# A sample's value products in one piece, or in four pieces spread over four units of the attention loop

## The chip, the cores and the metric

The kernel runs on one core of a Trainium2 chip. The metric is the device time of one execution, in microseconds (us). A core has a matrix engine (TensorE, PE in the profile, with its weight loads listed apart as PEld), three engines for elementwise work (VectorE or DVE, ScalarE or ACT, GpSimd or POOL), a queue engine (SyncE or SP), and 16 DMA engines. Each engine runs its own instructions strictly in order; between engines they wait on semaphores. TensorE writes only to PSUM, an accumulator memory of 8 banks of 2 KB per partition, which DVE and ACT read. SBUF is the working memory.

## The reference

One layer of a streaming encoder, run for a prompt of 2048 frames and for 8 samples of 16 new frames each. Attention has 8 heads of 64 channels. A prompt frame sees its own chunk of 64 frames and the 8 chunks before; a sample's frame sees 256 cached keys and the 16 new ones. What matters here, cut to its core:

```python
s = jnp.einsum("bqhd,bkhd->bhqk", qc, kc) * scale + bias
p = jax.nn.softmax(jnp.where(valid, s, NEG_INF), axis=-1)
att = jnp.einsum("bhqk,bkhd->bqhd", p, vc)          # the value products
...
y = jnp.concatenate([att, c], axis=-1) @ w_out      # c: the convolution branch
x = x + rmsnorm(y, g_mix_post)
```

Cross-attention into 256 memory tokens and a gated feed-forward layer follow, for both groups. The outputs are the new frames and the updated caches.

## The kernel before

The program goes through memory keys and values, the input projection with the convolution, attention, the output projection with cross-attention, and the feed-forward layer. The change is in attention (about 645 to 945 us).

The prompt is cut into 16 tiles of 128 frames. The loop of `attention` goes over 128 units, one for each head (8) and tile (16), and at unit i it issues, in this order:

- `scores` of unit i (L847): products of the tile's queries with up to five key blocks, in four matmuls, into one of two "s" places in PSUM. DVE adds the bias and finds the maximum (`softmax_band`, L761), ACT takes the exponential (L763). The first tiles of a head have fewer blocks: 128 columns for tile 0, 256 for tile 1 and so on, 640 from tile 4.
- `transp` of unit i - 4 (L864): the probabilities of that unit are transposed on TensorE, in groups of up to four blocks, each group into one of three "t" slots in PSUM (one bank each). ACT copies the group to its high part (L865), DVE subtracts to get the low part (L866); then the slot is free.
- `values` of unit i - 6, every fourth unit (L877): the value products of four tiles, 16 matmuls of 128 to 512 columns, into the single "o" place, emptied by ACT (L881) and DVE (L883).
- at some units, one step of `sample`: the attention of one of the 8 samples over all heads, written as a generator whose pieces end at each `yield`.

A sample's steps are: load cached keys, cached values and new values from SP (L768, L770, L772); transpose the keys in two steps (L780, copied by ACT at L781); POOL copies the new keys behind them (L783); scores (L794, eight heads at once in 128 rows) with softmax and a normalisation on POOL (L798); transposes of the probabilities (L803); and the value products (L812, L813). The value products go over four pairs of heads: for each pair there are two blocks of cached values and one of new values, and the moving operand, the probabilities of the pair, is only 32 columns wide. In the profile each pair takes four matmul instructions of L812 and two of L813, so a sample has 24. All four pairs share one "o" tile, which two copies on DVE empty (L815, L816) into `attS`.

A sample belongs to a head: sample h starts its steps at tile 0 of head h, and a step is taken at every second unit (2, 4, ... 14), for the last head at every unit from its sixth tile on (`SLAST`). The value products come at unit 14, in the last head at tile 9.

The order on each engine is not just the order of the code. A planner goes through the instructions when the program is built, in simulated time: on each engine the earliest instruction in the code whose inputs and places are ready goes first, so a step of a sample can be hoisted ahead of its unit or slip behind it. The order so found is then fixed. `issue_after` adds an order edge: instructions of the block come behind a named one on the same engine.

The output projection (`mixout`) begins with the sample tile, which needs `attS` complete: its high and low parts are made by `prep` (L1003, L1004) and multiplied at L289. Only then come the 16 prompt tiles. The weights of the output projection are loaded during the last head into places that attention gives up, among them a buffer of cached keys and one of cached values.

Of the kernel before, what the change touches and what calls it, by code (L numbers as in the profile page):

```python
# [8 lines left out]
F32 = mybir.dt.float32  # L9
# [8 lines left out]
P = 128  # L18
D = 1024
KC = D // P  # L20
NPT = 16
S_TILE = 16
H = 8
DH = 64
# [5 lines left out]
DEC_B = 8  # L30
DEC_S = 16
# [5 lines left out]
WEIGH = (122, 124)  # L37
FROM = 2
F2 = 2
SLAST = NPT * (H - 1) + 4  # L40
MID = 4
TR0 = [12, 8]
MM = [12, 14, 4, 6]
# [93 lines left out]
class Build:  # L137
# [605 lines left out]
    def attention(self):  # L743
        nc, A = self.nc, self.A
# [13 lines left out]
        def softmax_band(ps, w, bias, sm):  # L758
            z = self.t(pool, [P, W5], F32, "z", 6)
            nmx = self.t(pool, [P, 1], F32, "nmx", 12)  # L760
            nc.vector.tensor_tensor_reduce(out=z[:, :w], in0=ps, in1=bias, scale=-1.0, scalar=3e38,  # L761
                                           op0=ALU.add, op1=ALU.min, accum_out=nmx[:, :])
            nc.scalar.activation(z[:, :w], z[:, :w], AF.Exp, bias=nmx[:, :], scale=-1.0, accum_out=sm)  # L763
            return z

        def sample(s):
            kc = self.t(pool, [P, 2, 512], F32, "kc", 2)
            nc.sync.dma_start(kc[:, :, :], A["cache_att_k"][s].rearrange("(b p) d -> p b d", p=P))  # L768
            vc = self.t(pool, [P, 2, 512], F32, "vc", 2)
            nc.sync.dma_start(vc[:, :, :], A["cache_att_v"][s].rearrange("(b p) d -> p b d", p=P))  # L770
            vn = self.t(pool, [DEC_S, 512], F32, "vn", 2)
            nc.sync.dma_start(vn[:, :], self.vsamp[s * DEC_S:(s + 1) * DEC_S, :])  # L772
            yield
            kt = self.t(pool, [P, 4, PAST + DEC_S], F32, "kt", 1)
            for c2 in range(0, 4, 2):
                pt = self.t(ps_t, [P, 2, 2, P], F32, "t")
                for c in range(2):
                    for b in range(2):
                        cc = slice((c2 + c) * P, (c2 + c + 1) * P)
                        nc.tensor.transpose(pt[:, c, b, :], kc[:, b, cc], self.ident[:, :])  # L780
                nc.scalar.copy(kt[:, c2:c2 + 2, :PAST].rearrange("p c (b k) -> p c b k", k=P), pt[:, :, :, :])  # L781
                yield
            nc.gpsimd.tensor_copy(kt[:, :, PAST:], self.ksamp[:, :, s * DEC_S:(s + 1) * DEC_S])  # L783
            yield
            qb = qbds[s % 2]
            for o in range(2):
                rr = slice(o * DH, (o + 1) * DH)
                nc.vector.tensor_copy(qb[rr, :, o * DEC_S:(o + 1) * DEC_S],
                                      self.qsamp[rr, :, s * DEC_S:(s + 1) * DEC_S])
            qb = qb[:, :, :].rearrange("p c x -> p (c x)")  # L790
            n = PAST + DEC_S
            ps = self.t(ps_s, [P, 2, 512], F32, "s")[:, 0, :n]
            for c in range(4):
                nc.tensor.matmul(ps, qb[:, c * P:(c + 1) * P], kt[:, c, :], start=c == 0, stop=c == 3)  # L794
            sm = self.t(pool, [P, 1], F32, "sm", 2)
            z = softmax_band(ps, n, bs[:, :], sm[:, :])
            nc.vector.reciprocal(sm[:, :], sm[:, :])
            nc.gpsimd.tensor_scalar(z[:, :n], z[:, :n], sm[:, :], None, ALU.mult)  # L798
            yield
            pt = self.t(ps_t, [P, 3, P], F32, "t")  # L800
            for b in range(3):
                w = P if b < 2 else DEC_S
                nc.tensor.transpose(pt[:w, b, :], z[:, b * P:b * P + w], self.ident[:, :])  # L803
            pp = self.t(pool, [P, 3, P], F32, "pp", 1)
            nc.scalar.copy(pp[:, :2, :], pt[:, :2, :])
            nc.scalar.copy(pp[:DEC_S, 2, :], pt[:DEC_S, 2, :])
            yield
            po = self.t(ps_o, [P, 4, 32], F32, "o")
            for c in range(4):
                cc, hc = slice(c * P, (c + 1) * P), slice(c * 32, (c + 1) * 32)  # L810
                for b in range(2):
                    nc.tensor.matmul(po[:, c, :], vc[:, b, cc], pp[:, b, hc], start=b == 0, stop=False)  # L812
                nc.tensor.matmul(po[:, c, :], vn[:, cc], pp[:DEC_S, 2, hc], start=False, stop=True)  # L813
            ss = slice(s * DEC_S, (s + 1) * DEC_S)
            nc.vector.tensor_copy(self.attS[:DH, :, ss], po[:DH, :, :DEC_S])  # L815
            nc.vector.tensor_copy(self.attS[DH:, :, ss], po[DH:, :, DEC_S:])  # L816

        def load_head(h):

            jj, odd = h // 2, h % 2  # L820
            rr = slice(odd * DH, (odd + 1) * DH)
            q2 = self.t(pool, row, F32R, f"q2{odd}", 1)
            k2 = self.t(pool, row, F32R, f"k2{odd}", 1)
            kl = self.t(pool, row, F32R, f"kl{odd}", 1)
            v2 = self.t(pool, [P, NPT, P], F32R, f"v2{odd}", 1)
            nc.gpsimd.dma_start(q2[:, :], self.qs[jj][rr, :, :].rearrange("d c n -> (d c) n"))
            for c, dst in ((0, k2), (1, kl)):
                nc.gpsimd.dma_start(dst[:, :], self.ks[jj][c, rr, :].unsqueeze(1).to_broadcast([DH, 2, NPT * P]))
            nc.gpsimd.dma_start(v2[:, :, :], self.vs[h // 4][:, h % 4, :, :])
            bt = self.t(pool, [P, W5], F32, "bt", 2)  # L830
            nc.sync.dma_start(bt[:, :], toep[h][:, :])
            nc.gpsimd.memset(bt[:DH, W5 - DH:], NEG)
            nc.gpsimd.memset(bt[DH:, :DH], NEG)
            return q2, k2, kl, v2, bt
# [15 lines left out]
        def transp(zs, t, quad):  # L850
            if t % 4 == 0:
                quad = [self.t(pool, [P, 20, P], F32R, f"p{c}{t // 4 % 2}") for c in "hl"]
            ph, pl = quad
            if t < 4:
                chunks = [(5 * t + 4 - t, 5 * t + 5)]
            else:
                x = t % 4
                chunks = [(4 * x, 4 * x + 4)] + ([(16, 20)] if x == 3 else [])
            for a, b in chunks:
                pt = self.t(ps_t, [P, 4, P], F32, "t")  # L860
                for x in range(a, b):
                    u = t - t % 4 + x // 5
                    k = x % 5 - max(0, 4 - u)
                    nc.tensor.transpose(pt[:, x - a, :], zs[u][:, k * P:(k + 1) * P], self.ident[:, :])  # L864
                nc.scalar.copy(ph[:, a:b, :], pt[:, :b - a, :])  # L865
                nc.vector.tensor_tensor(pl[:, a:b, :], pt[:, :b - a, :], ph[:, a:b, :].bitcast(F32), ALU.subtract)  # L866
            return quad
# [24 lines left out]
        for _ in range(2):  # L892
            qb = self.t(pool, [P, 4, P + 2 * DEC_S], F32, "qbd")
            nc.gpsimd.memset(qb[:, :, :], 0.0)
            qbds.append(qb)
        fill = iter(())
        self.wo_load = self.out_weights()
        zq, quads = {}, {}
        n = len(units)
# [2 lines left out]
        for i in range(n + LV + 1):  # L902
            if i < n:
                h, t = units[i]
                if t == 0:
                    fill = sample(h)
                if t == 6 and h + 1 < H:
                    heads[h + 1] = load_head(h + 1)
                zq[h, t] = scores(heads[h], t, self.sums[:, t, h:h + 1])
            u = i - LT  # L910
            if 0 <= u < n:
                h, t = units[u]
                quads[u // 4] = transp({x: zq.get((h, x)) for x in range(t - t % 4, t + 1)}, t, quads.get(u // 4))
            u = i - LV
            if 0 <= u < n and u % 4 == 3:
                h, t = units[u]
                values(h, heads[h], t - 3, quads.pop(u // 4))
            if i % NPT and (i % 2 == 0 or i > SLAST):
                next(fill, None)
            if i == n - NPT:  # L920
                self.selectors()
            if i in WEIGH:
                for _ in self.weigh(WEIGH.index(i), ps_t, "t"):
                    pass
            if i in (n - 13, n - 11, n - 9, n - 7):
                next(self.wo_load)
# [771 lines left out]
```

## Time and profile before

| | before |
|---|---|
| median of 3 runs | 3012.31 us (3011.44 to 3014.95) |
| the profiled execution, its own time | 3017.42 us |
| its span, first to last instruction | 3015.6 us |
| TensorE busy | 2946.0 us (98%) |
| weight loads busy | 2712.9 us (90%) |
| DVE / ACT / POOL busy | 71% / 45% / 47% |
| mean granted TensorE clock | 0.989 |
| matmuls at L812 / L813 / L864 | 128 / 64 / 560 |

The profile is of one execution. A busy TensorE in it is not TensorE at its peak, since matmuls are pipelined and their ends are modelled; two things tell more: the share of the weight loads, and the granted clock, which falls to one half in some stretches. A row of a group names the line, the engine, the operation, what it writes and reads with their shapes, the count after an x, the busy time with the mean length of one in ns, and the engine's idle time just before them with what ended it. A row of waits names who waited for whom, the sum in us, how often, and the longest. A row in order of time has the start, the length, and the instructions merged in it.

### The profile page before, as it was taken

What the parts mean: (1) busy time and instruction counts of PE and PEld (TensorE: products, weight loads), DVE (VectorE), ACT (ScalarE), POOL (GpSimd) and SP (SyncE); (2) the same over time, 40 slices, a digit from 0 to 9 for tenths busy, and PEclk for the clock granted to TensorE, in tenths of its full rate; (3) what the DMA queues carried; (4) which work ended last, traced back from release to release, by engine and by line L of the source; (5) the groups of instructions that cost most, each with busy time, mean ns of one, the idle gap of its engine ahead of it and who ended that gap; (6) DMA issues with size and microseconds to landing.
All of it is one profiled execution on the core that took longest, in us unless ns stands there. A gap on an engine that the chain in (4) does not pass through costs nothing.

```text
span 3015.6 us, 46098 instructions
## 1 busy us (share of the span) xinstructions
PE 2946.0 (98%) x16924; PEld 2712.9 (90%) x16924; DVE 2137.0 (71%) x3086; ACT 1358.3 (45%) x2729; POOL 1418.9 (47%) x1338
## 2 busy tenths in 40 slices
PE   7999999979999999999999999999999999999998
PEld 7999999969998888788878999999999999888887
DVE  6697795857786466535357887888788999655566
ACT  4535365657785345323334333433334444433433
POOL 1267496721113234226356655555555775524413
PEclk9999999989899999999999999999999999999999
DMA  8635353644534556324246433444434445756674
GB/s 295 246 112 179 96 165 110 202 167 172 181 135 153 175 190 216 128 68 147 74 166 210 138 128 132 166 166 153 154 125 160 144 139 187 260 187 207 220 230 149
DMA packets 197695, 500.10 MB, mean 166 GB/s; under 512 B 19349, under 2 KB 84765, under 8 KB 188627
## 3 DMA queue, kind: packets, MB, share of 16 engines
q1 hardware_dynamic: 182539, 427.53, 42.9%
q0 software_dynamic: 14928, 69.61, 6.2%
q8 instruction: 133, 2.18, 0.3%
q14 instruction: 95, 0.78, 0.1%
HBM read 365.97 MB, written 141.81 MB: 168 GB/s over the span
## 4 chain that ended last, share of the span: by engine, by line
PE 38%; DMA 4%; DVE 3%; issue 3%; POOL 3%; ACT 0%; SPq 0%; DVEq 0%; POOLq 0%; ACTq 0%
PE psb L283 12%; PE psb L282 12%; PE psb L281 12%; DMA sbf<-in_w_down_dram 2%; POOL sbf L1538 1%; PE psb L289 1%; DMA sbf<-x 1%; PE psb L1393 1%; DVE sbr L1416 0%; DMA sbf<-in_w_gate_dram 0%; DVE sbr L1608 0%; POOL sbf L338 0%; DMA hn<-sbf 0%; DVE sbr L1542 0%; DVE flexb L1478 0%
## 5 line engine op out<-in xcount | busy, mean ns | idle before, releaser
L281 PE MATMUL psb<-sbr 128*128 128x384 f32 (+3 forms) x2808 | 942.6, 337 | 4.1 <-DVE flexb L426 1.4
L282 PE MATMUL psb<-sbr 128*128 128x384 f32 (+3 forms) x2356 | 806.2, 342 | 3.4 <-DVE sbr L318 3.3
L283 PE MATMUL psb<-sbr 128*128 128x512 f32 (+3 forms) x1848 | 632.8, 344 | 3.7 <-DVE sbr L1608 3.6
L281 PEld LDWEIGHTS psb<-sbr 128*128 128x128 f32 x2808 | 530.9, 189 | 33.9 <-DVE flexb L426 2.1
L283 PE MATMUL psb<-sbr,sbx 128*128 128x384 f32 (+2 forms) x1484 | 477.2, 322 | 0.0
L282 PEld LDWEIGHTS psb<-sbr 128*128 128x128 f32 x2356 | 445.5, 189 | 30.6 <-DVE sbr L318 3.6
L283 PEld LDWEIGHTS psb<-sbr 128*128 128x128 f32 x1848 | 348.0, 189 | 33.2 <-DVE sbr L1608 6.3
L289 PE MATMUL psb<-sbr 128*128 128x512 f32 x1200 | 295.3, 394 | 2.7 <-POOL sbr L1251 1.4
L1416 DVE TENSOR_TENSOR sbr<-sbf,sbr 128x512 fp32r<-128x512 f32 x258 | 262.5, 1020 | 38.6 <-ACT sbr L1415 37.7
L1415 ACT CAST sbr<-sbf 128x512 fp32r<-128x512 f32 x258 | 159.3, 620 | 278.7 <-PE psb L282 228.8
L283 PEld LDWEIGHTS psb<-sbr,sbx 128*128 128x128 f32 x1484 | 281.2, 190 | 0.1
L523 DVE SCALAR_TENSOR_TENSOR psb<-sbf,psb 128x768 f32<-128x768 f32 (+1 forms) x290 | 264.3, 911 | 6.2
L289 PEld LDWEIGHTS psb<-sbr 128*128 128x128 f32 x1200 | 222.2, 189 | 48.5 <-POOL sbr L1251 1.8
L1608 DVE TENSOR_TENSOR sbr<-sbf,sbr 128x384 fp32r<-128x384 f32 (+2 forms) x242 | 166.4, 711 | 93.6 <-ACT sbr L1607 92.4
L276 POOL TENSOR_TENSOR sbx<-sbf,sbr 128x1024 fp32r<-128x1024 f32 x62 | 158.7, 2563 | 79.9 <-ACT sbr L275 76.4
L1607 ACT CAST sbr<-sbf 128x384 fp32r<-128x384 f32 (+2 forms) x242 | 112.4, 483 | 171.6 <-PE psb L282 149.4
L1538 POOL TENSOR_TENSOR sbf<-sbf 128x512 f32<-128x512 f32 x77 | 107.0, 1392 | 165.5 <-DMA sbf<-in_w_down_dram 163.6
L533 POOL TENSOR_TENSOR flexb<-flexb,flexb 128x128 f32<-128x128 f32 (+1 forms) x180 | 169.4, 942 | 23.1 <-ACT flexb L532 12.3
L281 PE MATMUL psb<-sbr,sbx 128*128 128x384 f32 (+1 forms) x524 | 170.6, 327 | 1.5 <-ACT sbx L1415 0.8
L1415 ACT CAST sbx<-sbf 128x512 fp32r<-128x512 f32 x153 | 94.7, 620 | 162.2 <-PE psb L282 147.4
L1416 DVE TENSOR_TENSOR sbx<-sbf,sbx 128x512 fp32r<-128x512 f32 x153 | 155.3, 1016 | 16.3 <-ACT sbx L1415 16.0
L1410 POOL TENSOR_TENSOR sbf<-sbf 128x512 f32<-128x512 f32 x66 | 96.9, 1468 | 107.3 <-DVE sbr L1416 50.5
(339 smaller groups left out, 6269.2 us busy)
## 6 DMA issues: line engine op xcount, KB each, us to landing
af<-flexb SPq DMA_DIRECT2D x33, 1344.0 KB, 5.7
sbf<-in_w_down_dram SPq DMA_DIRECT2D x154, 256.0 KB, 3.8
sbf<-in_w_gate_dram SPq DMA_DIRECT2D x66, 512.0 KB, 3.5
sbf<-in_w_up_dram SPq DMA_DIRECT2D x66, 512.0 KB, 3.9
sbf<-af SPq DMA_DIRECT2D x85, 384.0 KB, 4.1
sbf<-x SPq DMA_DIRECT2D x49, 512.0 KB, 4.0
sbf<-in_w_in_dram SPq DMA_DIRECT2D x48, 512.0 KB, 4.1
sbr<-ks POOLq DMA_DIRECT2D x16, 1024.0 KB, 8.5
```

The costliest lines, as they stand in the source:

```text
L276: self.lo_engine.tensor_tensor(lo[:, :], wf[:, :], hi[:, :].bitcast(F32), ALU.subtract)
L281: nc.tensor.matmul(ps, lh, rh, start=start, stop=False, **kw)
L282: nc.tensor.matmul(ps, lh, rl, start=False, stop=False, **kw)
L283: nc.tensor.matmul(ps, ll, rh, start=False, stop=stop, **kw)
L289: nc.tensor.matmul(y[o], l, r[:, o * 512:(o + 1) * 512], start=start and x == 0, stop=stop and x == 2)
L523: nc.vector.scalar_tensor_tensor(acc if w < CW - 1 else o, src(w), cwt[:, j, w:w + 1], acc, ALU.mult, ALU.add)
L533: nc.gpsimd.tensor_tensor(o, o, v, ALU.add)
L1415: nc.scalar.copy(hs[j][:, :], src[j])
L1416: nc.vector.tensor_tensor(ls[j][:, :], src[j], hs[j][:, :].bitcast(F32), ALU.subtract)
L1538: nc.gpsimd.tensor_tensor(acc[:, :], acc[:, :], q[:, :], ALU.add if s > 0 else ALU.subtract)
L1607: nc.scalar.copy(ch[:, m], a[:, x, m])
L1608: nc.vector.tensor_tensor(cl[:, m], a[:, x, m], ch[:, m].bitcast(F32), ALU.subtract)
```

## The change

The value products of a sample are cut into four parts, one per pair of heads, and each part is a step of its own. A part has its own accumulator of 32 columns, and it is no longer in the "o" place but takes the next of the three "t" slots, which it shares with the transposes. It is put behind the last transposes that were issued so far (`last_turn`), and two copies on DVE, a quarter as wide as before, empty it.

The steps of sample s are now taken at fixed units counted from the first unit of its head: 1, 7, 8, 9, 11, 13, 14, 15 and 16, the same for every head. The four parts come at 13, 14, 15 and 16; the last one is in the first unit of the next head, and for the last sample it is in the first pass of the loop after all scores. The load of the cached values moves from the first step to the end of the second transposes, and POOL's copy of the new keys joins that step, since one `yield` is gone.

```diff
-SLAST = NPT * (H - 1) + 4
+SAMPLE_AT = (1, 7, 8, 9, 11, 13, 14, 15, 16)
...
-            vc = self.t(pool, [P, 2, 512], F32, "vc", 2)
-            nc.sync.dma_start(vc[:, :, :], A["cache_att_v"][s].rearrange("(b p) d -> p b d", p=P))
             vn = self.t(pool, [DEC_S, 512], F32, "vn", 2)
...
-                yield
+                if c2 == 0:
+                    yield
             nc.gpsimd.tensor_copy(kt[:, :, PAST:], self.ksamp[:, :, s * DEC_S:(s + 1) * DEC_S])
+            vc = self.t(pool, [P, 2, 512], F32, "vc", 2)
+            nc.sync.dma_start(vc[:, :, :], A["cache_att_v"][s].rearrange("(b p) d -> p b d", p=P))
             yield
...
-            po = self.t(ps_o, [P, 4, 32], F32, "o")
+            ss = slice(s * DEC_S, (s + 1) * DEC_S)
             for c in range(4):
                 cc, hc = slice(c * P, (c + 1) * P), slice(c * 32, (c + 1) * 32)
-                for b in range(2):
-                    nc.tensor.matmul(po[:, c, :], vc[:, b, cc], pp[:, b, hc], start=b == 0, stop=False)
-                nc.tensor.matmul(po[:, c, :], vn[:, cc], pp[:DEC_S, 2, hc], start=False, stop=True)
-            ss = slice(s * DEC_S, (s + 1) * DEC_S)
-            nc.vector.tensor_copy(self.attS[:DH, :, ss], po[:DH, :, :DEC_S])
-            nc.vector.tensor_copy(self.attS[DH:, :, ss], po[DH:, :, DEC_S:])
+                po = self.t(ps_t, [P, 32], F32, "t")
+                with self.tc.issue_after(self.last_turn.ins):
+                    for b in range(2):
+                        nc.tensor.matmul(po[:, :], vc[:, b, cc], pp[:, b, hc], start=b == 0, stop=False)
+                    nc.tensor.matmul(po[:, :], vn[:, cc], pp[:DEC_S, 2, hc], start=False, stop=True)
+                nc.vector.tensor_copy(self.attS[:DH, c, ss], po[:DH, :DEC_S])
+                nc.vector.tensor_copy(self.attS[DH:, c, ss], po[DH:, DEC_S:])
+                if c < 3:
+                    yield
...
-                    nc.tensor.transpose(pt[:, x - a, :], zs[u][:, k * P:(k + 1) * P], self.ident[:, :])
+                    self.last_turn = nc.tensor.transpose(pt[:, x - a, :], zs[u][:, k * P:(k + 1) * P],
+                                                         self.ident[:, :])
...
-                if t == 0:
-                    fill = sample(h)
...
-            if i % NPT and (i % 2 == 0 or i > SLAST):
-                next(fill, None)
+            for s in range(DEC_B):
+                if i - NPT * s in SAMPLE_AT:
+                    next(samples.setdefault(s, sample(s)), None)
```

More of the change, by code (lines that the diff above doesn't have):

```diff
@@ L895, in attention @@
             qbds.append(qb)
-        fill = iter(())
+        samples = {}
         self.wo_load = self.out_weights()
```

## The prediction

> **What bounds the kernel now.** I read the page's slices first, because they place the edited stage; this row is the clock that TensorE was granted, in tenths of full speed, over 40 equal slices.
>
> ```profile
> PEclk9999999989899999999999999999999999999999
> ```
>
> The ninth and the eleventh slice (603 to 679 and 754 to 829 us) are the only ones under nine tenths, and they lie at the start of the attention loop and in it. Next, the sums over the steady part of that loop (columns: length, then PE, weight loads, DVE, ACT and POOL busy with their counts, granted clock, DMA share, GB/s) and what PE waited for in it.
>
> ```profile
> 676.00:945.00 269.00, 267.13 (x1750) 248.31 (x1751) 205.15 (x481) 205.88 (x469) 41.18 (x58) 0.94 0.43 155
> PE psb L877 <- DVE sbf L883: 1.4, 1, 1.4
> ```
>
> PE is busy 267 of 269 us and its longest wait is 1.4 us, while DVE and ACT are each free for about 64 us. So PE sets the pace here, and anything that makes PE slower costs time directly. The clock of 0.94 says what does: six stretches at half clock. They stand first below, with two full-clock stretches for comparison.
>
> ```profile
> 685.32:692.15 6.83, 6.83 (x27) 6.17 (x28) 2.00 (x6) 2.07 (x6) 0.29 (x2) 0.50 1.05 406
> 722.87:726.28 3.41, 3.41 (x14) 3.02 (x15) 1.77 (x6) 1.24 (x3) 0.29 (x2) 0.50 0.72 252
> 757.00:760.41 3.41, 3.41 (x17) 3.31 (x16) 2.34 (x6) 1.92 (x5) 0.29 (x2) 0.50 0.90 330
> 787.72:794.54 6.82, 6.82 (x28) 6.30 (x29) 2.68 (x8) 2.38 (x6) 0.29 (x2) 0.50 0.74 279
> 821.85:828.68 6.83, 6.83 (x29) 6.34 (x29) 2.96 (x8) 3.06 (x7) 0.29 (x2) 0.50 0.89 339
> 917.42:920.84 3.42, 3.42 (x16) 3.34 (x16) 2.88 (x12) 2.72 (x7) 0.00 (x0) 0.50 0.48 153
> 692.15:717.00 24.85, 24.85 (x174) 23.40 (x174) 21.51 (x50) 21.57 (x49) 3.50 (x6) 1.00 0.34 113
> 828.68:852.00 23.32, 23.32 (x162) 22.06 (x162) 19.39 (x49) 19.06 (x45) 3.50 (x6) 1.00 0.24 80
> ```
>
> All lengths are 3.41 us or twice that, so the clock is decided in windows of 3.41 us: nine windows, 30.72 us in all. To see what decides, I compared the forms of the matmuls in two windows. After the first (681.91 to 685.32, sample 0) the clock was halved; after the second (855.98 to 859.39, sample 5) it was not.
>
> ```profile
> L812 PE MATMUL psb<-sbf,flexb 128*128 128x32 f32 x9 | 1.5, 278 | 0.0
> L847 PE MATMUL psb<-sbr 128*128 128x256 f32 x6 | 1.2, 302 | 0.0
> L813 PE MATMUL psb<-sbf 16*128 16x32 f32 x4 | 0.8, 282 | 0.0
> L864 PE MATMUL psb<-ident,flexb 128*128 128x128 f32 x4 | 0.7, 286 | 0.0
> L847 PE MATMUL psb<-sbr 128*128 128x128 f32 x2 | 0.4, 302 | 0.2 <-DVE flexb L761 0.2
> ```
>
> ```profile
> L812 PE MATMUL psb<-sbf,flexb 128*128 128x32 f32 x9 | 1.5, 281 | 0.0
> L813 PE MATMUL psb<-sbf 16*128 16x32 f32 x6 | 1.2, 282 | 0.0
> L847 PE MATMUL psb<-sbr 128*128 128x512 f32 x2 | 0.7, 447 | 0.0
> L864 PE MATMUL psb<-ident,flexb 128*128 128x128 f32 x4 | 0.6, 272 | 0.0
> L847 PE MATMUL psb<-sbr 128*128 128x384 f32 x2 | 0.6, 379 | 0.0
> ```
>
> Count by width: 9x32 + 6x256 + 4x32 + 4x128 + 2x128 = 2720 columns in the window that was followed by half clock, and 9x32 + 6x32 + 2x512 + 4x128 + 2x384 = 2784 in the one that was not. My reading is that a window with too few streamed columns halves the next one, with the border near 2750. The sample's value products (L812 and L813) are 24 matmuls of only 32 columns, and they run in one burst. The rows of PE in order around the burst of sample 6:
>
> ```profile
> 885.73 0.63 PE L864 MATMUL psb<-ident,flexb 128*128 128x128 f32 x4
> 886.11 0.59 PE L847 MATMUL psb<-sbr 128*128 128x128 f32 x3
> 886.54 0.60 PE L864 MATMUL psb<-ident,flexb 128*128 128x128 f32 x4
> 886.89 0.71 PE L847 MATMUL psb<-sbr 128*128 128x256 f32 x4
> 887.45 0.60 PE L864 MATMUL psb<-ident,flexb 128*128 128x128 f32 x4
> 887.80 0.60 PE L847 MATMUL psb<-sbr 128*128 128x384 f32 x2
> 888.23 0.53 PE L812 MATMUL psb<-sbf,flexb 128*128 128x32 f32 x4
> ...
> 891.71 0.66 PE L864 MATMUL psb<-ident,flexb 128*128 128x128 f32 x4
> ```
>
> The burst lasts 891.71 - 888.23 = 3.48 us, as long as a window, for 24x32 = 768 columns. Where it fills a window, the clock falls.
>
> **The change part by part.** *Splitting the products.* PE's work stays: 24 matmuls per sample, now four parts of six, each 3.48 / 4 = 0.87 us, each held behind the transposes of its own unit. From 885.73 to 888.23 PE streams 512+384+512+1024+512+768 = 3712 columns in 2.50 us, 1485 per us, and this is a lean place, with the short scores of the next head. A window with one part has 3.41 - 0.87 = 2.54 us left for this and holds 2.54 x 1485 + 192 = 3964; one with two parts has 1.67 us left and holds 1.67 x 1485 + 384 = 2864. Both lie above 2784, the second by little, so I expect most drops to go and a few to stay.
>
> What the drops cost: the six stretches held 27+14+17+28+29+16 = 131 matmuls. At full clock 174+162 = 336 took 48.17 us, 6.98 per us, so 131 would take 18.8 us. Loss now: 30.72 - 18.8 = 12.0 us, or 1.33 us per window. Gain if all go: -12.0. I leave two windows, one in the first head, where PE is also held by other work, and one in the last, where no further head fills the units: +2.7. Bounds: none left, 0, and all nine left, +12.0.
>
> [...]
>
> *Accumulators in the three "t" slots instead of "o".* The parts now rotate with the transposes, whose slots are released by ACT's copy and DVE's subtraction. Rows for what a slot wait costs now, for the copies that empty an accumulator, and for the time to land of a cache load:
>
> ```profile
>   DVE sbr L866: 0.3, 1
> DVE sbf L815 <- PE psb L813: 12.8, 7, 3.7
> L815 DVE COPY sbf<-psb x8: 206/216/218, 688.4 to 917.4; 64x64 f32<-64x64 f32 x8
> DMA to landing us min/median/max: 3.5/4.5/5.8
> ```
>
> The transposes waited 0.3 us in one case for a slot. Four more users per sample bring a slot back a place earlier, but the part itself adds 0.87 us to the turn. I take +0.6 us, twice the 0.3, being nearest that row. Bounds: 0, since the shared "o" slot is given up in return and may repay it, and 32 parts at about 0.25 us, the length of one copy, +8.
>
> *Copies out.* 64 instead of 16, a quarter as wide; no row shows 16 columns, so each lies between 0 and 0.22 us. The 48 added ones cost at most 48 x 0.22 = 10.6 us of DVE, hidden by DVE's 64 free us; without that cover, +10.6. DVE waits for each part with the next scores' reduction (L761) queued behind, and ACT's exponential behind that; it now waits 12.8 us for seven bursts and would wait for shorter pieces. Taken at 0.
>
> *Loads and moved steps.* The key and new-value loads go a unit earlier. The value load goes behind the transposes and POOL's key copy; on SP it is held by its buffer until the sample two before has finished its last part, so it still lands (4.5 us) most of a head before use, and the next head's bias table behind it on SP has as long. For samples 0 and 1 the buffer is free early. POOL's copy is in one step with the second transposes; POOL is busy 41 of 269 us. Score and softmax move one unit earlier with two units still between them and the probabilities' transposes. All 0; if a first value load were late, at most its 5.8 us.
>
> *The last sample.* Its products finished with tile 9 of the last head; now the last part follows the transposes of tile 12. The output projection begins with the sample tile and needs them. Rows of the tail:
>
> ```profile
> 921.74 1.17 PE L289 MATMUL psb<-sbr 128*128 128x512 f32 x4
> ...
> 925.81 4.82 PE L289 MATMUL psb<-sbr 128*128 128x512 f32 x20
> ...
> 932.11 0.60 PE L864 MATMUL psb<-ident,flexb 128*128 128x128 f32 x4
> ```
>
> These 24 projection matmuls, 1.17 + 4.82 = 6.0 us, run before the transposes of tile 12 (932.11) and fill PE while the head drains. They will have to come after. The four parts, 3.48 us, move into the place: 6.0 - 3.5 = +2.5 us of hole. Bounds: 0, if tile 12 simply comes earlier, and +6.0.
>
> *Sum.* -12.0 + 2.7 + 0.6 + 0 + 2.5 = -6.2 us. The profiled execution took 3017.4 us, 5.1 above the median of 3012.3, with drops whose places depend on where the windows fall; I apply the difference to the median: 3006.1, and say 3006.
>
> **The rivals.** *The waits eat it (about the same).* The slots cost the +8: -12.0 + 2.7 + 8 + 2.5 = +1.2, 3013.5. For it: a slot is released only when DVE is through, and DVE is busy 205 of 269 us. Against: the 0.3 us above.
>
> *The parts bunch (no effect).* If the order of issue lets parts pile up behind a late transpose, windows still fill and the drops stay: +0.6 + 2.5 = +3.1, 3015.4. Against: each part is held behind a different unit.
>
> *The clock falls more often (slower).* The four parts spread over some 7 us with transposes and short scores between. If such windows fall under the border, two per sample follow at half clock: 8 x 6.83 = 54.6 us, a loss of 54.6 x 12.0 / 30.72 = 21.3 instead of 12.0, so +9.3 + 0.6 + 2.5 = +12.4, 3024.7. It decides once a two-part window streams under 2750 columns; 2864 is near. It would be certain if transposes did not count: of the 3712 columns 1536 are theirs, leaving 870 per us, 1.67 x 870 + 384 = 1840 in a two-part window against 2720 - 512 = 2208 in the one that halved. [...]
>
> *Everything goes and the tail closes.* -12.0, 3000.
>
> **How the numbers follow.** 0.2%, 6 us, is about what a measurement can tell from no change. Forecast, with 3002 to 3006 most likely of it and the clean gain to 3000: 0.53. Waits eat it, or the forecast lands short of 6 us: 0.27. Parts bunch: 0.08. Slower: 0.12. So faster 0.53, same 0.35, slower 0.12. The range runs from 2999 (the clean gain, 1 us spare) to 3015 (bunched): about 0.12 lies above, 0.06 below.
>
> **What would show it.** Right: no stretch of 0.50 between 692 and 900 us or at most two, windows with at most 12 narrow matmuls, PE near 100% busy, the loop about 10 us shorter. Waits of L864 or the parts on DVE's copies would show the first rival; stretches of 0.50 over 40 us in sum, the slower one; a gap on PE of over 3 us after the last transposes, a worse tail. A reordered loop with PE idle in it, which I cannot see from here, would make the whole sum wrong.

## The result, and the profile after

The changed kernel took 3021.04 us (median of seven runs, 3019.56 to 3025.03), the kernel before, in turns with it on the same chip, 3012.09 us (seven runs, 3010.07 to 3018.95). The ratio is 1.0027 (1.0015 to 1.004): slower by 9 us, outside the predicted range and of the other sign.

The first row of the page to compare is the granted clock in 40 slices, for the changed kernel:

```profile
PEclk9999999989998999999999999999999999999999
```

The slice from 754 to 829 us is repaired, and there is a new low one, the thirteenth (907 to 982 us). To see this in numbers I cut both traces at the same matmuls, counted from the start: number 4200 lies in the first head, number 5700 near the start of the last, number 6050 in the output projection. Sums over the two stretches, of before and then of after (columns as in the prediction):

```profile
666.33:894.48 228.15, 225.63 (x1501) 210.86 (x1501) 175.39 (x421) 175.97 (x410) 29.34 (x53) 0.94 0.45 161
894.48:954.77 60.29, 60.03 (x352) 52.10 (x351) 47.18 (x87) 42.45 (x85) 16.61 (x11) 0.97 0.41 140
```

```profile
666.31:885.91 219.60, 216.90 (x1502) 198.74 (x1501) 179.52 (x462) 175.53 (x409) 26.94 (x52) 1.00 0.46 164
885.91:957.12 71.21, 67.31 (x351) 57.49 (x351) 48.31 (x96) 43.32 (x89) 19.29 (x13) 0.88 0.38 130
...
913.25:916.67 3.42, 2.08 (x15) 1.66 (x13) 3.29 (x3) 1.68 (x4) 2.35 (x1) 1.00 0.00 0
916.67:933.74 17.07, 16.73 (x63) 14.75 (x64) 10.26 (x20) 8.27 (x13) 2.37 (x1) 0.50 0.57 199
```

The loop is 8.6 us shorter, without any half clock; the last head and the start of the output projection are 10.9 us longer, with one stretch of half clock of 17.07 us, five windows, begun by a window in which PE was busy for only 2.08 of 3.42 us. The rows of PE there, in order:

```profile
913.27 0.61 PE L868 MATMUL psb<-ident,flexb 128*128 128x128 f32 x4
913.72 0.53 PE L815 MATMUL psb<-sbf,flexb 128*128 128x32 f32 x4
914.17 0.40 PE L816 MATMUL psb<-sbf 16*128 16x32 f32 x2
914.51 0.86 PE L882 MATMUL psb<-sbr 128*128 128x128 f32 x3
917.01 1.11 PE L868 MATMUL psb<-ident,flexb 128*128 128x128 f32 x4 [1.64 <-DVE sbr L871]
...
920.07 0.90 PE L815 MATMUL psb<-sbf,flexb 128*128 128x32 f32 x4
...
923.75 0.90 PE L815 MATMUL psb<-sbf,flexb 128*128 128x32 f32 x4
...
927.45 0.90 PE L815 MATMUL psb<-sbf,flexb 128*128 128x32 f32 x4
...
931.97 2.23 PE L289 MATMUL psb<-sbr 128*128 128x512 f32 x5
```

In the order of the program's text the transposes are now L868, the parts L815 and L816, the prompt's value products L882. The eighth sample's four parts lie between 913.72 and 929 us, and not one matmul of the output projection (L289) comes before 931.97. In the kernel before (a second trace of it, introduced below) the same place reads:

```profile
913.52 1.18 PE L289 MATMUL psb<-sbr 128*128 128x512 f32 x4
...
917.61 4.79 PE L289 MATMUL psb<-sbr 128*128 128x512 f32 x20
...
923.33 0.70 PE L289 MATMUL psb<-sbr 128*128 128x512 f32 x2
...
926.00 2.45 PE L289 MATMUL psb<-sbr 128*128 128x512 f32 x10
```

These 36 stood in the drain of the last head. All belong to the sample tile, which takes 48 of them (six for each of eight pieces of the weights). They are 512 columns wide; what is left in their place are transposes of 128, parts of 32 and the prompt's value products of 128 to 512.

The wait of 1.64 us in the low window can be followed to its cause. DVE's subtraction (L1008, one of `prep`, for the convolution half of the sample tile) ran beside a subtraction of POOL (L276), and DVE's release of a "t" slot (L871) stood behind it; the last row groups 17 such L1008:

```profile
913.47 2.89 DVE L1008 TENSOR_TENSOR sbr<-flexb,sbr 128x512 fp32r<-128x512 f32 x1
916.28 0.68 DVE L871 TENSOR_TENSOR sbr<-psb,sbr 128x512 fp32r<-128x512 f32 x1
```

```profile
913.45 2.35 POOL L276 TENSOR_TENSOR sbr<-sbf,sbr 128x1024 fp32r<-128x1024 f32 x1 [3.85 <-PE psb L851]
```

```profile
L1008 DVE TENSOR_TENSOR sbr<-flexb,sbr x17: 673/693/2886, 913.5 to 1179.4; 128x512 fp32r<-128x512 f32 x17
```

Its median is 693 ns; 2886 is POOL's 2.35 us and then one of its own length, less 0.15. POOL's was first by 0.02 us. In the first traces of the two kernels this subtraction occurs 68 times (L1004, L1008). The eight that took over 2 us (2.44 to 2.89) all began while POOL was in an instruction of 1024 columns (L276; L1047 before, L1051 after), and ended 0.55 us after it; the three that began 0.09 to 0.22 us ahead of such a one took 0.68 to 0.69 us. This long subtraction is not new. In the second trace of the kernel before it is L1004:

```profile
916.37 2.89 DVE L1004 TENSOR_TENSOR sbr<-flexb,sbr 128x512 fp32r<-128x512 f32 x1
```

There PE had matmuls of L289 to run meanwhile and lost at most 0.3 us in the whole tail. In the run without the dependency, below, its like takes 2.87 us too, and L289 runs beside it. What is new in the changed kernel is that PE has nothing else to do meanwhile.

### The profile page after: what moved, and what is told of

Read it like the earlier page. It is cut to its first block, busy times and chain, and to the rows that moved or that the text cites. A ratio compares the mean times of both kernels' runs of the same rounds, so it can differ in the third digit from the quotient of the medians.

```text
span 3023.2 us, 46142 instructions
## 1 busy us (share of the span) xinstructions
PE 2945.7 (97%) x16924; PEld 2706.7 (90%) x16924; DVE 2144.3 (71%) x3134; ACT 1359.4 (45%) x2729; POOL 1420.8 (47%) x1338
## 4 chain that ended last, share of the span: by engine, by line
PE 38%; DMA 4%; DVE 3%; issue 3%; POOL 2%; ACT 0%; SPq 0%; POOLq 0%; DVEq 0%; ACTq 0%
PE psb L283 12%; PE psb L282 12%; PE psb L281 12%; DMA sbf<-in_w_down_dram 2%; PE psb L289 2%; POOL sbf L1542 1%; DMA sbf<-x 1%; PE psb L1397 1%; DMA sbf<-hn 0%; DMA sbf<-in_w_gate_dram 0%; DVE sbr L1612 0%; DVE sbr L1420 0%; POOL sbf L338 0%; DVE sbr L1546 0%; DVE sbx L1420 0%
## 5 line engine op out<-in xcount | busy, mean ns | idle before, releaser
L289 PE MATMUL psb<-sbr 128*128 128x512 f32 x1200 | 296.3, 395 | 1.9 <-ACT sbr L1290 1.1
L289 PEld LDWEIGHTS psb<-sbr 128*128 128x128 f32 x1200 | 223.0, 189 | 48.1 <-ACT sbr L1290 1.3
L276 POOL TENSOR_TENSOR sbx<-sbf,sbr 128x1024 fp32r<-128x1024 f32 x62 | 158.8, 2564 | 78.5 <-ACT sbr L275 74.7
```

The source lines that it names most:

```text
L276: self.lo_engine.tensor_tensor(lo[:, :], wf[:, :], hi[:, :].bitcast(F32), ALU.subtract)
L289: nc.tensor.matmul(y[o], l, r[:, o * 512:(o + 1) * 512], start=start and x == 0, stop=stop and x == 2)
```

## The experiments

Each was run in turns with the kernel before, which had medians of 3012.37, 3012.77 and 3013.59 us in the three sets of runs; ratios are against the one beside it.

**The last sample, added alone.** The kernel before, with the eighth sample alone as in the changed kernel (units 1, 7, 8, 9, 11, 13 to 16, four parts; `sample_split` is the changed kernel's `sample`):

```diff
-                    fill = sample(h)
+                    fill = sample(h) if h < H - 1 else iter(())
...
+            if i == NPT * (H - 1):
+                late = sample_split(H - 1)
+            if i - NPT * (H - 1) in SAMPLE_AT:
+                next(late, None)
```

> The kernel before with only the last sample as in the changed one: samples 0 to 6 keep their bursts, sample 7 is in four parts at units 13 to 16 of the last head. Theory A: the loss alone, 3019 to 3025 us, with several windows at half clock after 910 us and the drops of samples 0 to 4 still there. Rival B: within 3 us of before, 3009 to 3015 us.

3018.88 us, ratio 1.0022 (1.001 to 1.0033). The last head and tail, and the half clock in it:

```profile
887.04:955.48 68.44, 65.00 (x352) 56.39 (x352) 46.55 (x93) 41.96 (x86) 18.94 (x12) 0.90 0.34 118
917.35:931.00 13.65, 13.65 (x55) 12.47 (x55) 7.29 (x16) 6.98 (x10) 1.54 (x1) 0.50 0.52 195
```

The last sample alone costs 6.5 us of the 9, in the place expected.

**The last sample, taken out of the change.** The reverse: the changed kernel with the eighth sample as before (`sample_burst` is the `sample` of the kernel before, `LAST_AT` its units 2, 4, 5, 6, 7, 8 and 9).

```diff
+                last = s == DEC_B - 1
-                if i - NPT * s in SAMPLE_AT:
-                    next(samples.setdefault(s, sample(s)), None)
+                if i - NPT * s in (LAST_AT if last else SAMPLE_AT):
+                    next(samples.setdefault(s, sample_burst(s) if last else sample(s)), None)
```

> The changed kernel, with the eighth sample alone as it was before: its value products in one burst in the "o" place at tile 9 of the last head, its steps at units 2, 4, 5, 6, 7, 8 and 9 of that head. Theory A (the split repairs the loop, and the last sample gives it all back in the tail): the part from the last head's scores to the output projection takes 59 to 62 us with at most 4 us of half clock, as before; the loop ahead of it stays at about 220 us without half clock; the time is 3006 to 3010 us, below the kernel before. Rival B (what is lost is not the last sample's, but the new order of the loop or its load of the value cache shifts all that follows): 3017 us or more.

3015.62 us, ratio 1.001 (1.0 to 1.002). The time lies between the two theories. Its loop, and its last head and tail:

```profile
666.90:885.88 218.98, 216.61 (x1501) 198.79 (x1501) 179.71 (x462) 175.67 (x409) 26.94 (x52) 1.00 0.46 165
885.88:949.85 63.97, 62.16 (x352) 53.69 (x352) 47.46 (x90) 43.17 (x87) 19.91 (x13) 0.95 0.39 141
```

So 5.4 us of the 9 come back (3021.04 - 3015.62), but it stays 2.9 above the kernel beside it. The run above gives 6.5 for the same step, so some two thirds of the loss are the last sample's. The loop is as short as in the changed kernel; the tail is still some 3.7 longer than before (63.97 against 60.29), and the projection then waits, in one case 1.9 us, for DVE to empty an accumulator:

```profile
PE psb L290 <- DVE flexb L1104: 2.1, 2, 1.9
PE psb L935 <- ACT sbr L923: 1.0, 1, 1.0
```

Why the planner's order comes out worse there, with the last sample as before, is open.

**Is it the dependency?** The sample tile of the projection no longer reads the samples' attention:

```diff
-                att = self.attS[:, :, :]
+                att = ct[:, :, :]
```

> The changed kernel, but the sample tile of the output projection reads the convolution half in the place of the attention half, so the samples' attention is still computed in full and not used: nothing of the output projection waits for the last part any more. Theory A2 (the loss is that the sample tile has to wait for the last part, and its 24 matmuls are missing where the last head drains): the sample tile starts near 912 to 922 us, the tail takes 59 to 62 us with at most 4 us of half clock, and the time is 3006 to 3011. Rival A1 (the narrow parts alone starve the windows): the half clock in the tail stays at 10 us or more, and the time at 3016 or more.

3014.31 us, ratio 1.0005 (0.9995 to 1.0014), and no half clock left from the loop to the tail:

```profile
665.41:884.60 219.19, 216.63 (x1501) 198.72 (x1501) 179.48 (x462) 175.65 (x409) 26.95 (x52) 1.00 0.45 165
884.60:948.51 63.91, 59.89 (x351) 50.61 (x351) 45.89 (x96) 42.60 (x87) 20.31 (x13) 1.00 0.40 141
...
L289 PE MATMUL psb<-sbr x48: 387/392/497, 909.0 to 934.8; 128*128 128x512 f32 x48
```

The parts are as narrow and as late as in the changed kernel, but L289 starts at 909 us and runs among them. So the half clock in the tail comes from the projection's matmuls being held back by the dependency. The tail still has 4.0 us without a matmul (63.91 - 59.89) where before had 0.3, so it is 63.9 and not the 59 to 62 expected, and the time was 3 us above the window expected.

**The last sample's steps earlier.** The changed kernel, its eighth sample moved forward, four parts at units 9 to 12:

```diff
+LAST_AT = (2, 4, 5, 6, 8, 9, 10, 11, 12)
...
-                if i - NPT * s in SAMPLE_AT:
+                if i - NPT * s in (SAMPLE_AT if s < DEC_B - 1 else LAST_AT):
```

> The changed kernel with only the last sample's steps earlier: loads at unit 2 of the last head, keys at 4 and 5, scores at 6, probabilities at 8, the four parts at 9, 10, 11 and 12 (as changed: 13 to 16). Theory A, the last sample: the change gains about 8 us in the loop and loses about 11 us after the last scores, because the parts and the sample tile of the output projection come too late there; with the parts early the 17 us at half clock around 917 to 934 us are gone or down to one window, the projection's first matmul comes by 924 us, and the time is 3003 to 3010 us. Rival B, the split itself (slots shared with the transposes, 48 more copies, a reordered loop) is what costs: the time stays at 3017 us or more.

3020.15 us, ratio 1.0028 (1.0018 to 1.0038): a miss. The sample tile starts at 921.9 us and the half clock shrinks to one window in each of two stretches, but waits take its place. Last head and tail, and the stretch after it, which took 32.7 us in the changed kernel:

```profile
884.49:950.98 66.49, 61.49 (x351) 52.26 (x351) 47.02 (x95) 43.43 (x88) 17.89 (x12) 0.97 0.39 135
950.98:988.41 37.43, 34.70 (x151) 27.98 (x150) 14.70 (x24) 11.50 (x24) 12.40 (x17) 0.95 0.44 145
```

PE has 5.0 and 2.7 us without a matmul in them. What the tail loses is not the clock alone.

**The slots.** The changed kernel, its parts in the "o" place:

```diff
-                po = self.t(ps_t, [P, 32], F32, "t")
+                po = self.t(ps_o, [P, 32], F32, "o")
```

> The changed kernel with the four parts' accumulators in the single o place again, in place of the three t slots. If the shared slots cost anything (bound in the prediction: 8 us), this is faster than the changed kernel by that, 3013 to 3019 us. By theory A the slots cost next to nothing and the last sample is as late as before: 3019 to 3024 us; slower than the changed kernel where a part has to wait for the place that the four tiles' value products hold.

3021.83 us, ratio 1.003 (1.0019 to 1.0041): no gain. The loop took 217.0 us (219.6 with the "t" slots), the tail 70.2 against 71.2, but matmul 4200 came 2.9 us later (669.19 against 666.31), ahead of any part (the first is matmul 4299). So the loop is some 2 us shorter without the shared slots, and the whole time is not: by the medians the slots don't decide.

**Wider parts.** The changed kernel, each part streaming all 128 probabilities, of which the copies take what counts:

```diff
-                        nc.tensor.matmul(po[:, :], vc[:, b, cc], pp[:, b, hc], start=b == 0, stop=False)
+                        nc.tensor.matmul(po[:, :], vc[:, b, cc], pp[:, b, :], start=b == 0, stop=False)
```

> The changed kernel, with each part's matmuls streaming all 128 probabilities instead of 32; the copies take the two 16 columns that count, nothing else differs. Theory A1 (the tail's half clock comes from windows with few streamed columns): the 17 us of half clock in the tail shrink to 7 or less and the time falls to 3011 to 3016 us. Rival A2 (the tail loses time because the sample tile of the output projection comes late, whatever is streamed): half clock and time as in the changed kernel, 3019 to 3023.

3026.87 us, ratio 1.0044 (1.0031 to 1.0057). Both theories missed: slower than the changed kernel.

```profile
668.39:890.61 222.22, 219.81 (x1501) 198.81 (x1500) 179.85 (x462) 175.98 (x410) 27.30 (x53) 1.00 0.45 162
890.61:962.08 71.47, 65.14 (x352) 54.82 (x351) 48.77 (x96) 42.74 (x88) 20.67 (x13) 0.93 0.37 127
923.05:933.29 10.24, 10.24 (x37) 8.84 (x37) 3.81 (x9) 3.90 (x5) 0.00 (x0) 0.50 0.50 198
```

The half clock is shorter, 10.24 us in place of 17.07, as the columns say, but the tail is not: 6.3 us are without a matmul. In the loop, which had no half clock to lose, the wider parts cost 2.6 us.

**Columns, with the burst left whole.** The same widening in the kernel before, to 128 and to 64:

```diff
-            po = self.t(ps_o, [P, 4, 32], F32, "o")
+            po = self.t(ps_o, [P, 4, P], F32, "o")
...
-                    nc.tensor.matmul(po[:, c, :], vc[:, b, cc], pp[:, b, hc], start=b == 0, stop=False)
+                    nc.tensor.matmul(po[:, c, :], vc[:, b, cc], pp[:, b, :], start=b == 0, stop=False)
```

> The kernel before, bursts and all, but each value matmul of a sample streams all 128 columns of the probabilities in place of the 32 of its pair of heads; the accumulator has 4 times the columns, and the same two copies pick out those that are wanted. The burst streams 3072 columns in place of 768 and should take the same 3.5 us, since each matmul takes 0.145 us now and its weight load, not its 32 columns, sets that. Theory C, streamed columns decide the clock, border near 2750 in a window: no drop at any sample, 12 us less, 2999 to 3004 us. Rival D, something else in the burst decides (narrow matmuls as such, transposes, waits): the drops stay, 3010 to 3015 us, or more if wide matmuls take longer.

> The kernel before with the sample's value products streaming 64 probabilities instead of 32 or 128; the burst then holds 1536 columns. At 128 columns the loop had 3.4 us of half clock and the time was 0.9989 of before; the products took 172 ns each there against 145. If the border lies well above 1536 plus what fits beside it, half clock stays in the loop, 10 us or more, and the time is that of before, 3011 to 3014; if 64 columns are enough, the half clock goes and the products cost less than at 128: 3006 to 3009.

At 128 columns 3010.03 us, ratio 0.9989 (0.998 to 0.9997), faster than the kernel before; at 64, 3015.40, ratio 1.0011 (1.0001 to 1.0021). The loops of the two traces, 128 and then 64:

```profile
664.24:885.65 221.41, 218.85 (x1501) 200.77 (x1501) 175.59 (x423) 175.89 (x411) 29.39 (x53) 0.99 0.46 166
```

```profile
662.95:883.21 220.26, 217.66 (x1501) 202.47 (x1501) 174.38 (x421) 175.79 (x410) 29.43 (x53) 0.98 0.46 166
```

TensorE's matmuls come in the same order in these traces as in those of the kernel before; the burst left whole loses its half clock when more columns pass, so it was the columns. The one halved window left at 128 columns follows a wait of 1.5 us for DVE, in a window with PE busy for 1.93 of 3.42 us and with no burst in it. At 64 the traced execution still has two windows in the loop, and over its eleven runs the mean clock is 0.990, that of before: 1536 columns in a burst are not enough. At 128 the mean is 0.993, but the gain is 2 to 3 us and not the 8 to 13 expected. The kernel before had less to lose than its first trace showed (below), and the wider products take longer: from start to start 172 ns each in the trace against 145, which is 24 x 7 x 0.027 = 4.5 us for seven samples. So the weight load alone does not set their time.

**The kernel before and the changed one, once more.**

> The kernel before, unchanged, with a second trace of it. If the half-clock stretches are set by the program alone, the loop shows the same nine, 30.7 us; if where the windows fall decides, as the prediction supposed, other stretches show, and at a mean clock nearer to 0.990, the mean of the timed executions, than the 0.989 of the first trace there are 20 to 27 us in all.

> The changed kernel once more, for a second trace. Theory A: no half clock between matmuls 4200 and 5700, and 10 to 17 us of it in the last head and the tail, since the sample tile's products are missing there in every execution. If the first trace's 17.1 us was chance, 7 or less.

These executions took 3012.21 and 3021.22 us, each within 0.2 us of its median, so they are the fairer pair; each is a single execution. Loop and tail of before, with the half clock of its loop, and then of after:

```profile
664.22:886.26 222.04, 219.41 (x1502) 205.29 (x1501) 174.65 (x421) 176.01 (x410) 29.40 (x53) 0.97 0.46 165
886.26:946.54 60.28, 59.99 (x352) 52.11 (x351) 47.18 (x87) 42.44 (x85) 16.62 (x11) 0.97 0.39 140
...
683.83:690.66 6.83, 6.83 (x28) 6.24 (x29) 2.92 (x8) 2.39 (x6) 0.29 (x2) 0.50 1.04 399
721.37:724.78 3.41, 3.41 (x15) 3.03 (x15) 2.29 (x5) 2.18 (x5) 0.29 (x2) 0.50 0.56 183
816.95:820.36 3.41, 3.41 (x17) 3.35 (x16) 2.19 (x6) 2.94 (x7) 0.29 (x2) 0.50 1.04 407
```

```profile
664.64:883.57 218.93, 216.54 (x1502) 198.77 (x1501) 179.71 (x462) 175.68 (x408) 26.94 (x52) 1.00 0.46 165
883.57:954.77 71.20, 67.05 (x351) 57.35 (x351) 48.11 (x96) 43.32 (x89) 19.33 (x13) 0.88 0.37 130
```

The half clock in the loop of before is 13.7 us here and was 27.3 in the first trace, in the same program; the tail of after repeats its 71.2 us with 17.07 of half clock. The difference of the two traces' spans, 3019.4 - 3010.4 = +9.0 us, is made of -3.1 in the loop, +10.9 in the last head and tail, and +1.2 in all else. Over 77 timed executions of the kernel before, the mean clock was 0.990, and over seven of the changed one it was 0.990 too: as much half clock as before, in another place.

The two traces of before also price the half clock without any model: 228.15 - 222.04 = 6.1 us for 13.7 us of it, 0.45 us per us. The 13.7 us gone from the loop should then give 6.1 us, and it is 3.1. What weight loads (PEld) waited for between 695 and 883 us shows what came instead, before and then after:

```profile
PEld psb L877 <- DVE sbf L883: 1.7, 1, 1.7
PEld psb L847 <- DVE flexb L761: 0.7, 3, 0.3
```

```profile
PEld psb L851 <- DVE flexb L761: 3.2, 11, 0.4
PEld psb L868 <- DVE sbx L871: 3.2, 10, 0.4
```

Scores now wait for DVE's reduction of an earlier unit, and transposes for DVE to give back a "t" slot: 6.4 us in 21 short waits, against 2.4, a difference of the size of the missing 3. The rows of the loops say the same. The weight loads stood idle (length less busy) for 222.04 - 205.29 = 16.8 us before, and for 218.93 - 198.77 = 20.2 us after; with the parts in "o" it was 18.3.

**The moved steps alone.** The kernel with the last sample as before, the other seven on the new units, their products undivided at unit 14:

```diff
-SAMPLE_AT = (1, 7, 8, 9, 11, 13, 14, 15, 16)
+SAMPLE_AT = (1, 7, 8, 9, 11, 14)
...
-                po = self.t(ps_t, [P, 32], F32, "t")
-                with self.tc.issue_after(self.last_turn.ins):
+            po = self.t(ps_o, [P, 4, 32], F32, "o")
```

> The kernel with the last sample as before, and for the seven others the new units of the steps and the later load of the value cache (1, 7, 8, 9, 11), but their value products undivided, in one burst in the "o" place at unit 14. Against the kernel in which the same seven are divided too (3015.6 us). Theory S (the moved steps cost the 3 us above the kernel before, by a different order of all that follows): 3016 us or more here, since the half-clock stretches of the loop come back and the order stays. Theory P (the parts cost it, as they break up the groups of scores, transposes and prompt value products; at full clock matmuls 4200 to 5200 took 146.2 us with the parts against 143.8 in the second trace of before, half clock taken out): 3011 to 3014, and 143.5 to 144.5 us at full clock for these matmuls.

3013.66 us, ratio 1.001 (1.0001 to 1.0018; the medians differ by 0.1 us). The half clock is back in the loop, 27 us in this trace, and the tail is short again:

```profile
665.26:892.16 226.90, 225.44 (x1501) 211.18 (x1501) 174.05 (x424) 177.25 (x413) 29.25 (x53) 0.94 0.45 162
892.16:950.83 58.67, 58.38 (x352) 50.67 (x352) 45.74 (x83) 41.60 (x84) 16.68 (x12) 1.00 0.42 144
```

Matmuls 4200 to 5200 took 152.5 us with 20.5 of half clock, 143.3 to 144.5 without it (at 0.45 or 0.39 us per us), where the parts have 146.3. So the moved steps and the later load cost nothing by the medians, and less than 0.2% by the interval; the longer tail and the slower loop come with the parts.

**Two halves.** The kernel before with the first seven samples' products in two halves at units 14 and 15, in "o", the second behind its unit's transposes:

```diff
+            w = 4 if s == DEC_B - 1 else 2
+            for a in range(0, 4, w):
+                po = self.t(ps_o, [P, w, 32], F32, "o")
+                with self.tc.issue_after(self.last_turn.ins) if a else nullcontext():
...
-            if i % NPT and (i % 2 == 0 or i > SLAST):
+            if i % NPT and (i % 2 == 0 or i % NPT == NPT - 1 or i > SLAST):
```

> The kernel before with one part of the change only, in a milder form: for the first seven samples the value products go in two halves of two pairs of heads, in two "o" tiles at units 14 and 15, the second behind the transposes of its unit. Steps, loads and the last sample are as before. If it is the lack of columns in one window that halves the clock, a window holds at most half a burst (1.74 us) and the loop loses its half clock: 3006 to 3010 us. Theory P (breaking up costs as much as the clock gives back): 3011 to 3014, with no half clock in the loop.

3009.71 us, ratio 0.9989 (0.9979 to 1.0):

```profile
665.15:880.99 215.84, 214.16 (x1502) 199.36 (x1501) 177.15 (x439) 177.35 (x413) 28.22 (x53) 1.00 0.47 167
880.99:942.40 61.41, 59.94 (x353) 52.15 (x352) 45.17 (x86) 41.10 (x83) 19.13 (x13) 0.97 0.43 148
```

The loop is 6.2 us shorter than in the second trace of before, just the price of its 13.7 us of half clock: the weight loads' idle time there is 16.5 us against 16.8. The tail and the rest of this execution are 3.7 us longer, so 2.5 us of it show in the whole (3009.71 against 3012.21). This and the wide burst are the two versions with a median below both kernels, by about 0.1% against before; for the halves the interval reaches 1.0.

## Why the prediction was wrong, step by step

**The mechanism was right, its border was not.** In these traces a window with too few streamed columns (736 to 2816 in those that lost the clock, by the count in the last section) is followed by half clock: halving the burst or dividing it removes the drops from the loop (13.7 and 27.3 us in the two traces of before), widening it to 128 leaves 3.4 us of them, and undoing the division alone brings 27 us back. In the first trace of before PE was busy for 3.22 us or more of the 3.41 in the window ahead of each drop, and all through the halved ones, so waits of PE don't explain them. The slower rival's case of transposes that do not count is not borne out here: leaving them out, a window with 1184 columns kept the clock (at 846 us with the last sample added alone) and one with 2304 lost it (at 814 us in the second trace of before), PE busy throughout in both. The border near 2750 came from two windows; the last section has the count from all traces. The 2864 columns reckoned for a window with two parts came near once: in the two traces of the changed kernel the leanest window of the loop, at the first sample, held 2944, and every other one 3456 or more.

**-12.0 for the drops: the term was mis-sized.** Per window the price was too low (1.33 us; measured 0.45 x 3.41 = 1.53). Their number was too high: nine windows, eight of them in the loop, were counted in one execution that had more than the usual (clock 0.989, where the mean is 0.990). A second trace has four in the loop. The prediction saw that the profiled execution was 5.1 us above the median "with drops whose places depend on where the windows fall", and still took the whole loss from it and applied it to the median: it took away drops that the median run need not have. With the second trace, -6.1 for the loop would have stood there.

**+2.7 for two windows left: wrong place.** None was left in the loop; five stood in the tail, which had one.

**+0.6 for the slots and 0 for the copies: together about +3.** The sum of both shows in the weight loads' waits for DVE; some 2 us of it are the shared slots, by the run with the parts in "o". The single copy was sized right (at most 0.22 us; the two of a part have medians of 157 and 178 ns), and DVE did have time free. But the cover was judged by DVE's busy share over the whole stretch (now 179.7 of 218.9 us), while what counts is whether DVE is there when a place is wanted. The lower of the two bounds, 0, applied where products went in halves through "o".

**0 for loads and moved steps: not contradicted.** The run with the steps alone has the median of the kernel beside it; its interval leaves room for up to 5 us.

**+2.5 for the last sample: the step that failed.** It measured +6.5 us by adding it alone; in the tail's traces it is +8.1 (68.4 against 60.3) and with the other samples' parts +10.9. The prediction listed the rows, 24 projection matmuls of 6.0 us in the drain, and that they "will have to come after", but priced only the hole in PE's time, less the 3.5 us that the parts fill. It left out three things. The wide matmuls also held the clock in the drain: without them five windows at half clock, at 0.45 us per us some 6.1 us more than the one of before. A window at half clock passes fewer columns, so the drop kept itself going until L289 came: the first four of the five halved windows held 1568, 2080, 2240 and 1856 columns, the fifth, with the first matmuls of L289 in it, 3072. Second, 12 more matmuls of the same tile were held behind the 24: L289 began at 931.97 instead of 913.52, so 36 wide matmuls were missing over 18 us. Third, PE had 4.1 us without a matmul there (71.20 - 67.05) where before had 0.3; the longest of these waits, 1.62 us here and 1.64 in the first trace, is the one behind L1008. The prediction's own mechanism, applied to the tail, would have given the first: it was used for the loop alone, and the tail was reckoned in busy time. The bound of +6.0 was too low for the same reason.

Together, by the fairer pair: -3.1 in the loop (-6.1 of clock, +3 of waits), +10.9 in the tail (6.1 of clock, 3.9 of PE without a matmul, 0.9 left over) and +1.2 elsewhere make +9.0, where -6.2 was forecast. By this sum the clock gives in the loop what it takes in the tail, and the waits make most of the loss; 2.1 us of it are not traced to a cause.

**The rivals.** Of the forecast's cases the slower one had the right sign but the wrong place: its time, 3024.7, is near by luck, since it has the drops at the spread parts in the loop, where there is none. The waits that eat the gain were right in kind, +3 and not +8. Of the sign "a gap on PE of over 3 us after the last transposes, a worse tail" the worse tail came. The gap was 3.9 to 4.1 us in sum, in several waits of 1.64 us at most, and all ahead of the last transposes.

## What to carry to other kernels

Where the clock follows how full a window is, as it did here, ask of every edit what it takes out of each window, and above all out of the drain between two stages, where independent wide work is scarce: moving a small producer later there cost what its consumer was filling, 10.9 us in this tail. Take a count of chance events, such as drops of the clock, from several executions, or at least scale it to the median's time; one profile of the kernel before held 27.3 us of half clock in the loop, the other 13.7. Split no finer than the window asks for: two halves gave the whole gain in the loop (6.2 us), and four parts gave half of it back in waits for DVE (3.1 us left).

## What was not expected of the hardware

In the changed kernel's tail the halved clock fed itself. In the two traces of the changed kernel 17.1 us of it each follow one window with PE busy for 2.08 and 2.58 of 3.41 us, although PE was busy for 16.73 and 16.23 us of the halved stretch. Two halved windows together, an estimate of what one at full clock would have passed, held 3648 to 4320 columns in the first of these traces, more than any window at full clock that lost it (2816).

The same program drops at other places in each execution: 27.3 us of half clock in its loop in one trace, 13.7 in another, and 3003.9 to 3019.9 us of span in the timed executions.

And the border is not one number of columns near 2750. All fourteen traces were cut into windows of 3.413 us (the prediction's 30.72 us over its nine), in step with their half-clock stretches, from 664 to 960 us, and the columns of the matmuls that start in each were counted. Of the windows at full clock, 34 were followed by half clock, with 736 to 2816 columns; 1136 were not, with 2112 or more. So in these traces the clock always fell under 2112 columns and never over 2816; between, 13 fell and 21 did not, and what else counts there is open.
